# Other accumulation banks for the gate blocks of a feed-forward stage, and an up product placed one step earlier

## The chip, the cores and the metric

The kernel runs on one core of a Trainium2 chip. The time is that of one execution on the device, in microseconds (us), and the figure compared is the median of several executions. The engines of the core are called TensorE (PE in the profile, with its weight loads as PEld), VectorE (DVE), ScalarE (ACT), GpSimd (POOL) and SyncE (SP, which issues the DMAs).

## The reference

One encoder layer is applied to two token sequences of 256 and 512 tokens (768 rows, model width 1024) that share one set of weights, all in 32-bit floats. An input projection feeds three groups of heads, whose joined output goes through an output projection and a layer norm. The second half of the layer, on which the change bears, is

```
x = LN(alpha * x + mix)
h = silu(x @ w_gate) * (x @ w_up)          # 1024 -> 2816
y = LN(alpha * x + h @ w_down)             # 2816 -> 1024
```

with `alpha` the fourth root of 2. The result is the 768 x 1024 output, handed back as the two sequences.

## The kernel before

**Precision.** Each 32-bit operand is split in two reduced-precision parts, a high and a low one: ScalarE writes the high part (the cast of line 120), VectorE or GpSimd subtracts it from the source (line 121). Each product is three matmuls: high x high, high x low, low x high.

**Tiling of the feed-forward stage.** The 2816 hidden columns are 22 tiles of 128, taken as 11 pairs. The first pair (0) is computed plainly. For pairs 1 to 10 the four blocks of a gate or up product (two halves of the tokens by two tiles, over two halves of the model width) are computed with seven block products instead of eight, in Strassen's manner; they bear the numbers 1, 2, 6, 5, 7, 3, 4. `g1` to `g7` are the gate products of a pair, `u1` to `u7` the up products, `d1` to `d7` the seven products of the down projection, which run one pair behind. A gate or up product is 12 matmuls of 384 columns, a down product 9 matmuls of 512 columns: three token tiles t of three matmuls each. The last two pairs' down projection is done plainly at the end (`piece`, lines 1073 to 1094).

**Banks.** A PSUM bank holds one accumulation. `bank(i)` (line 925) gives banks 0 to 3 (tiles named `ff` in the profile), 4 and 5 (`sc`), 6 (`tp`) and 7 (`av`). In `gate_up` (lines 1007 to 1044) the three entries of `banks` are used so: the first holds products 1, 6, 7 and 4, which are added up one on the other; the second holds product 2; the third holds products 5 and 3. The up products get only two banks, 0 and 1, and then 5 and 3 share the second with product 2. Between two products in one bank the sum so far is taken out. Products 1, 6 and 5 are copied by ScalarE (`snap`, line 1031); products 2, 7 and 3 are read by VectorE, which adds such a copy (line 1040); product 4 of a gate is read by ScalarE's SiLU (line 943), product 4 of an up block by VectorE's multiplication with the SiLU (line 946). The next product may write the bank only when that read is done.
`down` (lines 1049 to 1067) uses banks 2, 3, 4 for products 1, 6, 7, 4 and banks 5, 6, 7 for products 2, 5, 3, one bank for each t, and VectorE adds each product onto `y` (line 1063).

**After an up block.** `gated` (line 945) multiplies and splits. When blocks 0, 1 and 3 are there (after u3), GpSimd forms `S1 = HB1 + HB3` (line 955), then new HB1 and HB0 (lines 956, 957), and after u4 new HB2 (line 959). ScalarE and VectorE split these into the `mix` tiles that the down products read (`gt_split`, and `gated_rest` after the pair).

**Order.** TensorE works strictly in the order written in the program, here the list `MIXED` (line 35), one pair after the other. The order on the other engines is not written out: a planner in the framework replays the program with its own model of durations and picks for each engine, among what is ready there, what stands earliest in the program. The order that it finds is then fixed, and each engine works it off in that order. After each product `op_done` (line 218) calls `pump`, which emits the next weight splits, in the order of `SPLIT_ORDER` (line 33), at most two after a gate or up product and none after a down product (`AHEAD`), behind the last line-1040 addition on VectorE. Five slots hold two split operands each; a slot is free when both of its products are done. Raw weights come in 512 KB loads through three buffers.

Of the kernel before, what the change touches and what calls it, by code (L numbers as in the profile page):

```python
# [31 lines left out]

SPLIT_ORDER = ("g1", "g2", "g6", "g5", "g7", "g3", "d1", "g4", "d2", "d6", "u1", "d5", "u2", "d7", "d3", "u6", "d4",
               "u5", "u7", "u3", "u4")
MIXED = ("g1", "g2", "g6", "g5", "g7", "g3", "d1", "g4", "d2", "u1", "d6", "u2", "d5", "u6", "d7", "u5", "d3",
         "u7", "d4", "u3", "u4")
OUT_ORDER = [6, 7, 2, 3, 4, 0, 1, 5]

# [26 lines left out]
def encoder_layer(ctx: ExitStack, tc, a, o):  # L65
# [35 lines left out]
    def run(main):  # L101
        for cost, f in main:
            catch_up(clock["now"])
            f()
            clock["now"] += cost
# [112 lines left out]
    def op_done(key, prod):  # L218
        n = w_tiles.pop((key, prod))[1]
        ops_done.add(n)  # L220

        while w_state["tail"] in ops_done and (w_state["tail"] + 1 in ops_done or w_state["tail"] == len(items) - 1):
            w_state["tail"] += 2
            w_state["free"] += 1
        if w_state.get("after") is None:
            pump()
        else:
            with tc.issue_after(w_state["after"]):
                pump(AHEAD[key[0]])
# [582 lines left out]
    def x1_block(name, m, k):  # L812
        if name in ("t3", "t4"):
            return mix[k + (4 if name == "t3" else 0)][:, m, :H2]
        return xb[name][:, m, k]
# [109 lines left out]
    def bank(i):  # L925
        if i < 4:
            return pff.tile([P, 512], F32, tag=f"p{i}", name="ff")
        return ps_one({4: "sc", 5: "sc", 6: "tp", 7: "av"}[i])
# [16 lines left out]
    def gated(i, src, p):  # L945
        V.tensor_tensor(out=HB[i], in0=src, in1=TH[i], op=ALU.mult)  # L946
        if p >= NP_ST:
            gt_split(4 * (p - NP_ST) + i, HB[i])
            return

        if i in (0, 2):
            gt_split(i // 2, HB[i])
        have.add(i)
        if i > 0 and {0, 1, 3} <= have and i != 2:
            G.tensor_tensor(out=S1, in0=HB[1], in1=HB[3], op=ALU.add)
            G.tensor_tensor(out=HB[1], in0=HB[0], in1=HB[1], op=ALU.subtract)
            G.tensor_tensor(out=HB[0], in0=S1, in1=HB[0], op=ALU.subtract)
        if len(have) == 4:
            G.tensor_tensor(out=HB[2], in0=HB[2], in1=HB[0], op=ALU.subtract)
            gt_split(2, HB[0])  # L960
            gt_split(3, S1)
            have.clear()
# [3 lines left out]
    def gated_rest():  # L966
        gt_split(4, HB[1])
        gt_split(5, HB[2])
        gt_split(6, HB[3])
# [37 lines left out]
    def gate_up(kind, p, banks):  # L1007
        st = {}

        def step(prod, k):  # L1010
            if k == 0 and prod < 3:
                st[prod] = bank(banks[prod - 1])[:, :H2]
                if prod == 2:
                    st[5] = st[2]
            elif k == 0 and prod == 5 and len(banks) > 2:
                st[5] = bank(banks[2])[:, :H2]
            b = st[{2: 2, 5: 5, 3: 5}.get(prod, 1)]
            w = w_tiles[(kind, p), prod][0]
            for wi, m in ((0, 0), (0, 1), (1, 0)):
                TE.matmul(b, lhsT=w[:, wi, k * P:(k + 1) * P], rhs=x1_block(x_name[prod], m, k),  # L1020
                          start=(prod in (1, 2, 5) and k == 0 and wi == 0 and m == 0), stop=(k == 3 and wi == 1), skip_group_check=prod in (6, 7, 4, 3))
            if k == 3:
                after(prod)
                op_done((kind, p), prod)

        def after(prod):
            use = silu if kind == "g" else lambda i, src: gated(i, src, p)
            out = TH if kind == "g" else HB
            if prod in (1, 6, 5):
                st["s", prod] = t = wk2.tile([P, H2], F32, tag="snap", name="snap", bufs=2)  # L1030
                snap = S.copy(out=t, in_=st[5 if prod == 5 else 1])  # L1031
                if prod == 6 and kind == "g":

                    with tc.issue_after(snap.ins):
                        use(0, out[0])
            elif prod == 4:
                use(2, st[1])
            else:
                i, b, other = {2: (0, 2, 1), 7: (3, 1, 5), 3: (1, 5, 6)}[prod]
                w_state["after"] = V.tensor_tensor(out=out[i], in0=st[b], in1=st["s", other], op=ALU.add).ins  # L1040
                if prod != 2 or kind == "u":
                    use(i, out[i])

        return lambda prods: [(0.48, lambda prod=prod, k=k: step(prod, k)) for prod in prods for k in range(4)]
# [4 lines left out]
    def down(p):  # L1049
        st = {}  # L1050

        def step(prod, t):
            if prod < 3:
                st[prod, t] = bank(2 + t if prod == 1 else 5 + t)
            b = st[1 if prod in (1, 6, 7, 4) else 2, t]
            w = w_tiles[("d", p), prod][0]
            for m, wi in ((0, 0), (0, 1), (1, 0)):
                TE.matmul(b, lhsT=gt_block(a_slot[prod], m)[:, t * P:(t + 1) * P], rhs=w[:, wi],  # L1058
                          start=(prod in (1, 2, 5) and m == 0 and wi == 0), stop=(m == 1),
                          skip_group_check=prod in (6, 7, 4, 3))  # L1060
            for dt, c in {1: ((0, lo_half),), 2: ((0, lo_half),), 6: ((0, hi_half),), 5: ((3, hi_half),),
                          7: ((3, hi_half),), 3: ((0, hi_half),), 4: ((3, lo_half),)}[prod]:
                V.tensor_tensor(out=y[t + dt][:, c], in0=b, in1=y[t + dt][:, c], op=ALU.add)
            if t == 2:
                op_done(("d", p), prod)

        return lambda prods: [(0.64, lambda prod=prod, t=t: step(prod, t)) for prod in prods for t in range(3)]
# [47 lines left out]
    run(first_pair())  # L1115
    gated_rest()
    for p in range(1, NP):
        g = gate_up("g", p, (0, 1, 7))
        if p <= NP_ST:
            part = {"g": g, "u": gate_up("u", p, (0, 1)), "d": down(p - 1)}  # L1120
            for m in MIXED:
                run(part[m[0]]((int(m[1]),)))
            if p < NP_ST:
                gated_rest()
        else:
            u = gate_up("u", p, (2, 3))
            run(g(PRODUCTS))
            run(u(PRODUCTS))
# [112 lines left out]
```

## Time and profile before

| | |
|---|---|
| time, 3 runs | median 894.96 us (894.76 to 895.37) |
| the profiled execution's own time | 893.65 us |
| its span in the profile | 891.9 us, so 1.75 us lie around the span |
| busy TensorE matmul, weight load | 848.9 us (95%), 761.2 us (85%) |
| busy VectorE, ScalarE, GpSimd | 647.6 us (73%), 421.9 us (47%), 380.5 us (43%) |
| matmul groups of `gate_up` (line 1020), first start to last | 393.8 to 851.0 us of the span |
| first gate product of pairs 1 to 10 starts at | 393.8, 443.0, 489.7, 537.4, 584.3, 632.9, 679.6, 727.1, 773.4, 821.8 us |

The profile is that of one execution. Its rows give for each instruction, or run of like instructions, when it started, how long the engine was busy with it, and where the engine sat idle just before, how long and what ended that idle time (`[1.51 <-DVE bv L946]`: 1.51 us, ended by the VectorE instruction of line 946 that writes `bv`). The 25 us steps of the page's overview hide stalls of one or two microseconds; the timeline of one engine shows them. The stage of the change is read pair by pair: from one first gate product to the next.

### The profile page before, as it was taken

How to read it: one execution, taken by the hardware profiler on the slowest of the kernel's cores; microseconds unless marked ns; L12 is line 12 of the kernel's file. 1: busy time of each engine (PE TensorE's matmuls, PEld its weight loads, DVE VectorE, ACT ScalarE, POOL GpSimd, SP SyncE). 2: the span in 40 equal slices, each digit the busy share in tenths (PEclk: the TensorE clock that was granted, in tenths of full speed). 3: DMA queues.
4: the chain of work that ended last, by engine and by line, in shares of the span. 5: the costliest groups of instructions: out<-in, count | busy, mean ns of one | idle time of the engine just before them, and what ended most of it. 6: DMA issues, size and time to landing. Idle time of an engine off the chain costs nothing. (4 is left out here: it accounts for less than half of the span.)

```text
span 891.9 us, 12951 instructions
## 1 busy us (share of the span) xinstructions
PE 848.9 (95%) x4811; PEld 761.2 (85%) x4811; DVE 647.6 (73%) x1168; ACT 421.9 (47%) x922; POOL 380.5 (43%) x320
## 2 busy tenths in 40 slices
PE   8999999999999998899999999989998999999996
PEld 6889897888987887798898998988897989898985
DVE  3564447576677568758888698878887888779577
ACT  3475476676665436544453434443434344344421
POOL 0670011100220148775564646456564465544235
PEclk9999999999999999999999999999999999999999
DMA  7830202011017202011212122122121212112222
GB/s 228 254 99 24 71 26 71 24 49 49 13 59 260 72 1 70 25 48 48 95 48 75 44 71 95 48 72 72 54 88 48 94 49 95 48 50 92 72 83 107
DMA packets 22160, 66.66 MB, mean 75 GB/s; under 512 B 3664, under 2 KB 5584, under 8 KB 22096
## 3 DMA queue, kind: packets, MB, share of 16 engines
q1 hardware_dynamic: 22096, 65.82, 21.9%
q8 instruction: 38, 0.62, 0.3%
q14 instruction: 26, 0.21, 0.1%
HBM read 62.67 MB, written 3.15 MB: 74 GB/s over the span
## 5 line engine op out<-in xcount | busy, mean ns | idle before, releaser
L121 DVE TENSOR_TENSOR w<-raw,w 128x512 fp32r<-128x512 f32 (+2 forms) x179 | 174.8, 994 | 56.1 <-ACT w L120 56.0
L120 ACT CAST w<-raw 128x512 fp32r<-128x512 f32 (+2 forms) x213 | 139.4, 676 | 124.2 <-PE sc L1058 41.2
L1020 PE MATMUL ff<-x,w 128*128 128x384 f32 x600 | 117.4, 348 | 19.6 <-DVE bv L946 16.9
L1020 PEld LDWEIGHTS ff<-x,w 128*128 128x128 f32 x600 | 109.5, 195 | 26.2 <-DVE bv L946 19.8
L1020 PE MATMUL ff<-mix,w 128*128 128x384 f32 x480 | 91.2, 338 | 1.9 <-ACT snap L1031 1.5
L1020 PEld LDWEIGHTS ff<-mix,w 128*128 128x128 f32 x480 | 84.4, 188 | 5.3 <-ACT snap L1031 3.1
L454 PE MATMUL mm<-xhi,w 128*128 128x512 f32 x320 | 79.0, 346 | 0.0
L175 POOL TENSOR_TENSOR raw<-raw 128x512 f32<-128x512 f32 x49 | 73.4, 1498 | 3.4 <-DVE w L121 0.7
L120 ACT CAST mix<-bv 128x384 fp32r<-128x384 f32 x62 | 31.8, 513 | 90.4 <-DVE bv L946 63.7
L121 POOL TENSOR_TENSOR w<-raw,w 128x512 fp32r<-128x512 f32 x34 | 49.8, 1473 | 55.7 <-ACT w L120 55.7
L433 PE MATMUL mm<-w,xhi 128*128 128x256 f32 x384 | 71.4, 286 | 0.0
L852 PE MATMUL mm<-w,mix 128*128 128x512 f32 x270 | 68.3, 399 | 1.5 <-ACT tt L696 0.8
L1020 PE MATMUL ff<-xt,w 128*128 128x384 f32 x360 | 67.7, 336 | 0.3 <-ACT snap L1031 0.3
L1020 PEld LDWEIGHTS ff<-xt,w 128*128 128x128 f32 x360 | 63.5, 188 | 2.1 <-ACT snap L1031 0.6
L121 DVE TENSOR_TENSOR mix<-bv,mix 128x384 fp32r<-128x384 f32 x62 | 55.1, 891 | 12.0 <-ACT mix L120 11.5
L631 POOL TENSOR_TENSOR mn<-mn,neghalf 128x1 f32<-128x1 f32 x24 | 13.7, 573 | 116.4 <-DVE mn L630 112.5
L175 POOL TENSOR_TENSOR ws<-raw 128x512 f32<-128x512 f32 x29 | 42.4, 1464 | 49.2 <-DMA raw<-in_w 44.9
L852 PEld LDWEIGHTS mm<-w,mix 128*128 128x128 f32 x270 | 49.2, 188 | 12.6 <-ACT tt L696 1.3
L433 PEld LDWEIGHTS mm<-w,xhi 128*128 128x128 f32 x384 | 58.1, 189 | 1.4 <-issue 0.9
L1058 PE MATMUL ff<-w,mix 128*128 128x512 f32 x216 | 55.7, 393 | 0.0
L454 PEld LDWEIGHTS mm<-xhi,w 128*128 128x128 f32 x320 | 49.0, 189 | 6.1 <-issue 0.7
L1058 PE MATMUL sc<-w,mix 128*128 128x512 f32 x189 | 53.8, 393 | 0.0
(234 smaller groups left out, 1777.8 us busy)
## 6 DMA issues: line engine op xcount, KB each, us to landing
raw<-in_w SPq DMA_DIRECT2D x95, 512.0 KB, 3.3
y<-in_x SPq DMA_DIRECT2D x6, 512.0 KB, 8.7
out_y<-y SPq DMA_DIRECT2D x12, 256.0 KB, 2.0
raw<-in_xT SPq DMA_DIRECT2D x7, 384.0 KB, 5.2
ln<-in_lng SPq DMA_DIRECT2D x2, 512.0 KB, 7.0
ln<-in_lnb SPq DMA_DIRECT2D x2, 512.0 KB, 7.6
rpb<-in_rpbs SPq DMA_DIRECT2D x32, 30.6 KB, 3.4
rpb<-in_rpbp SPq DMA_DIRECT2D x16, 59.6 KB, 2.8
```

What stands on the lines that cost most here:

```text
L120: S.copy(out=hi, in_=src)
L121: eng.tensor_tensor(out=lo, in0=src, in1=hi.bitcast(F32), op=ALU.subtract)
L175: G.tensor_tensor(out=out, in0=in0, in1=in1, op=f)
L433: TE.matmul(ps, lhsT=x[:, k, t * P:(t + 1) * P], rhs=w[:, wi, sl], start=(k == 0 and x is xhi and wi == 0), stop=(k == KT - 1 and x is xlo))
L454: TE.matmul(p, lhsT=w[:, wi, sl], rhs=x[:, k, c0:c1], start=(k == 0 and wi == 0 and x is x_hi), stop=(k == KT - 1 and wi == 1))
L631: G.tensor_tensor(out=mn[:, 7:8], in0=mn[:, 7:8], in1=neghalf[:, 0:1], op=ALU.pow)
L852: TE.matmul(ps, lhsT=mix[OUT_ORDER[i]][:, m, t * P:(t + 1) * P], rhs=w[:, wi, sl], start=(i == first and m == 0 and wi == 0), stop=(i == l ...
L1020: TE.matmul(b, lhsT=w[:, wi, k * P:(k + 1) * P], rhs=x1_block(x_name[prod], m, k), start=(prod in (1, 2, 5) and k == 0 and wi == 0 and m = ...
L1058: TE.matmul(b, lhsT=gt_block(a_slot[prod], m)[:, t * P:(t + 1) * P], rhs=w[:, wi], start=(prod in (1, 2, 5) and m == 0 and wi == 0), stop= ...
```

## The change

Two edits. The gate blocks of pairs 1 to 10 get the banks 7, 1, 0 in place of 0, 1, 7: products 1, 6, 7 and 4 now gather in bank 7, products 5 and 3 in bank 0, product 2 stays in bank 1. And in TensorE's order the first up product goes in front of the second down product. `SPLIT_ORDER`, the order in which weights are split, stays.

```diff
 MIXED = ("g1", "g2", "g6", "g5", "g7", "g3", "d1", "g4", 
-         "d2", "u1", "d6", "u2", "d5", "u6", "d7", "u5", "d3",
+         "u1", "d2", "d6", "u2", "d5", "u6", "d7", "u5", "d3",
          "u7", "d4", "u3", "u4")
...
     for p in range(1, NP):
-        g = gate_up("g", p, (0, 1, 7))
+        g = gate_up("g", p, (7, 1, 0))
```

## Rows read from the trace of the kernel before

**Rows 1.** Waits of TensorE: us in total, times, longest.
```profile
PE ff L1020 <- DVE bv L946: 16.9, 9, 2.2
PE ff L1020 <- ACT ffs L943: 2.1, 2, 1.3
PE ff L1020 <- ACT snap L1031: 1.7, 4, 1.1
PE mm L852 <- DVE w L121: 0.6, 1, 0.6
```
**Rows 2.** TensorE timeline, end of pair 1 into pair 2: start, busy, count, idle before.
```profile
439.24 2.25 PE L1020 MATMUL ff<-mix,w 128*128 128x384 f32 x12
443.00 4.49 PE L1020 MATMUL ff<-x,w 128*128 128x384 f32 x24 [1.51 <-DVE bv L946]
...
451.57 2.28 PE L1020 MATMUL ff<-mix,w 128*128 128x384 f32 x12
```
**Rows 3.** TensorE timeline, end of pair 2 into pair 3.
```profile
485.25 2.24 PE L1020 MATMUL ff<-mix,w 128*128 128x384 f32 x12
489.68 6.01 PE L1020 MATMUL ff<-x,w 128*128 128x384 f32 x24 [2.19 <-DVE bv L946]
...
499.97 2.38 PE L1020 MATMUL ff<-mix,w 128*128 128x384 f32 x12
```
**Rows 4.** TensorE's granted clock (PEclk) in a window just after that wait.
```profile
490.50:491.50 1.00, 1.00 (x5) 1.00 (x4) 0.27 (x1) 0.63 (x2) 0.60 (x1) 0.50 1.02 283
```
**Rows 5.** TensorE timeline, end of pair 6 into pair 7.
```profile
675.14 2.28 PE L1020 MATMUL ff<-mix,w 128*128 128x384 f32 x12
679.56 4.43 PE L1020 MATMUL ff<-x,w 128*128 128x384 f32 x24 [2.14 <-DVE bv L946]
...
689.76 2.37 PE L1020 MATMUL ff<-mix,w 128*128 128x384 f32 x12 [1.07 <-ACT snap L1031]
```
**Rows 6.** TensorE timeline, end of pair 9 into pair 10.
```profile
817.39 2.25 PE L1020 MATMUL ff<-mix,w 128*128 128x384 f32 x12
821.76 4.43 PE L1020 MATMUL ff<-x,w 128*128 128x384 f32 x24 [2.13 <-DVE bv L946]
...
830.24 2.28 PE L1020 MATMUL ff<-mix,w 128*128 128x384 f32 x12
```
**Rows 7.** VectorE timeline, end of pair 2.
```profile
486.21 2.48 DVE L121 TENSOR_TENSOR w<-raw,w 128x512 fp32r<-128x512 f32 x4
488.61 0.55 DVE L946 TENSOR_TENSOR bv<-bv,ffs 128x384 f32<-128x384 f32 x1
489.08 0.55 DVE L946 TENSOR_TENSOR bv<-ff,ffs 128x384 f32<-128x384 f32 x1
```
**Rows 8.** GpSimd timeline, start of pair 3.
```profile
495.13 1.32 POOL L957 TENSOR_TENSOR bv<-gs,bv 128x384 f32<-128x384 f32 x1
```
**Rows 9.** ScalarE timeline, start of pair 3.
```profile
496.49 0.51 ACT L120 CAST mix<-bv 128x384 fp32r<-128x384 f32 x1 [2.10 <-POOL bv L957]
...
499.03 0.52 ACT L120 CAST mix<-bv 128x384 fp32r<-128x384 f32 x1 [0.99 <-POOL bv L959]
499.45 0.47 ACT L1031 COPY snap<-ff 128x384 f32<-128x384 f32 x1
```
**Rows 10.** ScalarE timeline, start of pair 2.
```profile
449.93 0.51 ACT L120 CAST mix<-bv 128x384 fp32r<-128x384 f32 x1 [2.54 <-POOL bv L957]
450.35 0.47 ACT L1031 COPY snap<-ff 128x384 f32<-128x384 f32 x1
```
**Rows 11.** ScalarE timeline, pair 3, around the SiLU of product g4.
```profile
509.54 0.62 ACT L120 CAST w<-raw 128x512 fp32r<-128x512 f32 x1 [3.95 <-POOL raw L175]
510.06 0.48 ACT L943 ACTIVATE ffs<-ff 128x384 f32<-128x384 f32 x1
```
**Rows 12.** VectorE timeline, pair 3: the low half of u1's weights.
```profile
498.51 1.03 DVE L121 TENSOR_TENSOR w<-raw,w 128x512 fp32r<-128x512 f32 x1
```
**Rows 13.** Pair 3 whole: PE, PEld, DVE, ACT, POOL busy, PEclk, DMA share, GB/s.
```profile
489.68:537.42 47.74, 46.18 (x231) 42.61 (x231) 39.16 (x56) 19.79 (x39) 26.65 (x20) 0.96 0.20 67
```

More of the change, by code (lines that the diff above doesn't have):

```diff
@@ L34 @@
                "u5", "u7", "u3", "u4")
-MIXED = ("g1", "g2", "g6", "g5", "g7", "g3", "d1", "g4", "d2", "u1", "d6", "u2", "d5", "u6", "d7", "u5", "d3",
+MIXED = ("g1", "g2", "g6", "g5", "g7", "g3", "d1", "g4", "u1", "d2", "d6", "u2", "d5", "u6", "d7", "u5", "d3",
          "u7", "d4", "u3", "u4")
```

## The prediction

> **What bounds the kernel now.** I read the page first (TensorE 95% busy, so only its idle time can be won), then TensorE's waits, then its timeline at each change of pair, and last the timelines of VectorE, GpSimd and ScalarE there. In the feed-forward stage TensorE has one large wait: nine times, once at the end of each pair 1 to 9, the first gate product sits until VectorE has multiplied the last up block [rows 1]. The reason is the bank: g1 opens bank 0, and u4 has just been gathered in bank 0; the multiplication that reads it stands on VectorE behind four weight splits and the multiplication for u3 [rows 7]. The wait is 1.48 to 1.56 us where an odd pair ends (four times, the first shown [rows 2]) and 2.13 to 2.19 us where pairs 2, 4, 6, 8 and 9 end [rows 3, 5, 6]. After three of the five long waits the granted clock is 0.50, the level of 1.2 GHz [rows 4], and g1 with g2 take 6.0 instead of 4.4 us [rows 3, 5].
>
> The sum of the waits, 16.9 us, is not what the edit is worth. A better measure is the way from the start of u4 to the start of g7, in which u4, g1, g2, g6 and g5 run. Without any wait a product takes 2.12 us: g1 to g7 in pair 10 are 8.48 us for four [rows 6]. So the way is 10.6 us at least. It is 12.33 us into pair 2 [rows 2] and 12.18 to 12.27 into pairs 4, 6 and 8; 14.72 into pair 3 [rows 3], 14.62 into pair 7 [rows 5], 14.78 and 14.84 into pairs 5 and 9; 12.85 into pair 10 [rows 6]. That pairs 3, 5, 7 and 9 agree is the point to see: pair 7 had no low clock and yet is not earlier, since it then waited 1.07 us at g7 for ScalarE's copy of g6 [rows 5]. In pair 3 that copy ends at 499.92 and g7 starts at 499.97, close behind it [rows 3, 9]. So a second chain ends there at nearly the same time: VectorE's multiplications, GpSimd's combinations up to lines 957 and 959, ScalarE's casts of what these give, and behind them, in ScalarE's queue, the copy of g6 that g7 needs, because g7 adds onto g6 in the same bank [rows 7 to 9].
>
> **The change part by part.** *Banks.* Nothing is added: the same matmuls, copies, additions and SiLUs run. g1 now opens bank 7, which d3 used last; between d3 and g1 stand u7, d4, u3 and u4, more than 8 us, so its reading is long done, and the wait of g1 goes. Bank 0 is opened by g5 instead, three products (6.4 us) after g1. The multiplication ended at 489.63 in pair 3 [rows 7], and g5 would come at 485.25 + 4 x 2.12 = 493.7, so it does not wait. g2 stays in bank 1, which u3 left a product earlier.
> What is late next is the copy of g6. Lower bound of the gain: ScalarE's order stays, g7 starts at 499.97 as now, and nothing is won into pairs 3, 5, 7, 9. Upper bound: g7 comes 10.6 us after u4 everywhere. That is 4 x (14.74 - 10.6) = 16.6 us for the pairs 3 to 9, 4 x (12.25 - 10.6) = 6.6 for 2 to 8, and 2.25 for pair 10: 25.4 us.
> Which of them? The planner gives ScalarE the order by what is ready first in its own replay, and there too g1 loses its wait, so the copy of g6 becomes ready earlier by 1.5 to 2.3 us against the GpSimd chain, which hangs on u3 and VectorE and not on g1. Today the copy stands behind both casts in pair 3 [rows 9] and between them in pair 2 [rows 10]; the two are 2.54 us apart [rows 9]. In pair 2 it was ready when g6 ended, near 451.57 - 2.12 = 449.45, some 0.5 us ahead of the earlier cast's start; a shift of 1.7 us widens that. In pair 3 g6 ended near 489.68 + 5.9 + 2.1 = 497.7, 1.2 us behind the earlier cast's start; the shift there is the wait of 2.2 us and, where the replay has it too, 1.5 of slow clock. I take: in front of both. Then g7 is on time, and the copy of g5, which g3 needs, is next: it stands behind the line-957 cast (done at 497.00 in pair 3 [rows 9]) and, I assume, two weight casts of 0.52 us step each, so it is done near 498.4, and g3 is due at 485.25 + 12.7 = 498.0. That costs about 0.45 us in the five long cases, 2.3 us in all, and nothing in the short ones.
> *u1 in front of d2.* Without this edit d2's third tile, in bank 7, would come only 1.4 us after g4 and wait for g4's SiLU; now it comes 2.1 + 1.4 = 3.5 us after. u1 in its turn no longer waits for that SiLU, since bank 0 was left by g3: the two waits on line 943, 2.1 us in all, go [rows 1]. Against it: in pair 3 the SiLU ran at 510.06 to 510.54, because it stood behind a weight cast that waited for GpSimd's sums of freshly loaded weights [rows 11]. g4 ended near 508.4, so 2.1 us after; today that is inside the 3.5. If TensorE is 3.7 us earlier there and that cast is not, d2's third tile is due at 508.3 and waits 2.2 us, in pairs 3, 5, 7 and 9: 9 us at most, 0 if the SiLU is put in front of the cast. I take a third of it, 3 us, since the SiLU becomes ready earlier by as much as TensorE gains.
> *Weights.* u1 is needed 2.1 us sooner than its place in the split order gives. In pair 3 its split ended at 499.54 [rows 12] and it started at 510.60; with 2.1 for the move and 3.7 for the gain some 5 us remain. In even pairs the emission of three pairs of splits (u5 with u7, u3 with u4, g1 with g2) falls one or two steps later, as the slot of g4 and d2 is freed one product later. TensorE never waits for a split in this stage (the only such wait is in the output projection [rows 1]), so I cost this at nothing. The raw loads behind these splits keep their order; no wait of SP's queue is added. VectorE is busy 39 of 48 us in a pair [rows 13]; at 45 us it still fits.
> Sum: 16.6 + 6.6 + 2.25 + 2.1 - 2.3 - 3 = 22.2 us. The profiled execution took 893.65 us, span 891.9; it becomes 871.5. The median is 1.3 us above the profiled execution, so 873.
>
> **The rivals.** *A, the copy of g6 passes only the later cast.* In pairs 3 to 9 it ends at 496.49 + 0.51 + 0.47 = 497.5 [rows 9], the way is 12.2, and 2.5 us are won four times; into pairs 2 to 8 it ends as now at 450.82 [rows 10], the way is 11.6, 0.6 won four times; 1 in pair 10, 2.1 at the SiLU: 15.5 us, so 879.5. For it: in both kinds of pair the line-957 cast stands in front today.
> *B, ScalarE's order stays as it is.* The wait moves from g1 to g7 in pairs 3 to 9: 0 there, 2.5 into the even pairs, 1 and 2.1 as above. But TensorE then stands idle 4.1 us in one piece, and if the clock falls after each of these, as after three of five waits of 2.1 us, 1.6 us of slow matmuls [rows 3, 4] come four times on top, now behind the chain and not hidden by it: +0.8, so 895.8, no measurable change.
> The Trainium skill (PSUM — Partial Sum Buffer, section on engine and sequencer instructions) says that the queues of ScalarE, VectorE and GpSimd are strictly first in, first out. The trace agrees: the copy of g6, ready near 497.7 in pair 3, ran at 499.45 behind a cast that waited [rows 9]. By that rule alone, with the order unchanged, the outcome would be B's; it is the reason why freeing a bank need not free TensorE.
> *C, slower.* B's mechanism with a longer chain: the later emission puts g1's and g2's splits into the block of four that stands in front of the multiplication for u3 at the end of the even pairs [rows 7]. Two more are 1.25 us on the chain, with the slow clock 2.85 us, four times 11.4, less the 5.6 that B keeps: +5.8, so 901. It decides from 1.4 us a pair on.
> *D, no effect*: bank 7 comes free as late as bank 0 did. Its last reader is 8 us old; I see nothing for it. 895.
>
> **How the numbers follow.** Forecast 0.55 (867 to 877, the two assumed costs at nothing or at full), A 0.23 (877 to 882), B 0.12, C 0.07, D 0.03. The range is 866 to 889: it holds the forecast and A and leaves out most of B, C and D. What a measurement of this kernel can tell from no change is 0.2%, 1.8 us. Faster: 0.55 + 0.23 + 0.06 of B (with the clock held up) = 0.84; the same: 0.08; slower: 0.08.
>
> **What would show it.** Right: no wait of g1 on line 946; g7 about 10.6 to 11 us after u4; pairs of 44.5 to 45.5 us instead of 46.3 to 48.7; PEclk 1.00 at the changes of pair; no wait of u1 on line 943. On ScalarE the copy of g6 in front of both casts. For A or B: g7 waits on the copy, 1 to 4 us. Wrong: a new wait of d2 in `av` on line 943, a matmul of line 1020 waiting for a split, or ways from u4 to g7 that stay at 14.7.

## The result, and the profile after

The changed kernel takes 870.28 us (869.17 to 871.16) where the kernel before took 894.86 us in the same comparison: 0.9726 of it, interval 0.9709 to 0.9742. The forecast was 873.0 in a range of 866 to 889. The profiled execution went from 893.65 to 870.31 us, its span from 891.9 to 868.5.

TensorE's waits after the change (us in total, times, longest). The nine waits on line 946 of [rows 1] are gone, and so are the two on line 943; the new entry is the first line: five waits of a product in bank 7 (`av`) for VectorE's addition of line 1040.

```profile
PE av L1020 <- DVE ffs L1040: 3.6, 5, 0.8
PE ff L1020 <- DVE bv L1001: 1.7, 1, 1.7
PE ff L1020 <- ACT snap L1031: 0.5, 2, 0.3
```

TensorE's timeline, end of pair 2 into pair 3, to be held against [rows 3] (start, busy, idle before). From u4 in the first line to g7 in the third it is 10.56 us instead of 14.72, and g1 follows u4 after 2.08 us. The last line is g4 with the new wait.

```profile
483.27 2.24 PE L1020 MATMUL ff<-mix,w 128*128 128x384 f32 x12
485.35 2.28 PE L1020 MATMUL av<-x,w 128*128 128x384 f32 x12
...
493.83 2.24 PE L1020 MATMUL av<-mix,w 128*128 128x384 f32 x12
...
501.06 2.35 PE L1020 MATMUL av<-mix,w 128*128 128x384 f32 x12 [0.82 <-DVE ffs L1040]
```

Pairs 2 and 3 whole (the second answers to [rows 13]; busy PE, PEld, DVE, ACT, POOL, then PEclk): TensorE is busy without a gap in pair 2, the granted clock is 1.00, and VectorE is busy 43 of 45 us in pair 3.

```profile
441.33:485.35 44.02, 44.02 (x232) 41.14 (x232) 38.90 (x56) 19.84 (x38) 26.78 (x19) 1.00 0.22 72
485.35:530.41 45.06, 44.24 (x232) 41.17 (x232) 42.95 (x58) 19.54 (x38) 28.06 (x19) 1.00 0.21 71
```

ScalarE's timeline, start of pair 3, against [rows 9]: the copy of g6 (first line) now stands in front of the cast that waits for line 957. The last line is the SiLU of g4, which starts as g4 ends (503.41; compare [rows 11]).

```profile
492.14 0.47 ACT L1031 COPY snap<-av 128x384 f32<-128x384 f32 x1
...
494.85 0.52 ACT L120 CAST mix<-bv 128x384 fp32r<-128x384 f32 x1 [1.81 <-POOL bv L957]
495.27 0.47 ACT L1031 COPY snap<-ff 128x384 f32<-128x384 f32 x1
...
503.46 0.49 ACT L943 ACTIVATE ffs<-av 128x384 f32<-128x384 f32 x1 [0.54 <-PE av L1020]
```

Where the span's 23.4 us came from, from the starts of the products in both traces: the nine ways from u4 to g7 went from 120.8 to 94.3 us, 26.5 won; from g4 to u2, where the waits for the SiLU sat, 78.2 to 76.1, 2.1 won; from g7 to d1 39.4 to 38.9, 0.5 won; from d1 to g4 19.2 to 23.8, 4.6 lost. Pair 1 lost 0.9 between g1 and g7, where g2 waited 1.7 instead of 0.7 us for the first pair's line 1001; in a second profile of the changed kernel it waits 0.7 again, so this loss is that execution's. The rest, 0.4 lost, is the later start of the stage, in this execution too.

### The profile page after: what moved, and what is told of

The parts are those of the page before. It is cut to its first block, busy times and chain, and to the rows that moved or that the text cites. A ratio compares the mean times of both kernels' runs of the same rounds, so it can differ in the third digit from the quotient of the medians.

```text
span 868.5 us, 12944 instructions
## 1 busy us (share of the span) xinstructions
PE 841.2 (97%) x4811; PEld 756.5 (87%) x4811; DVE 664.5 (77%) x1168; ACT 422.0 (49%) x922; POOL 387.6 (45%) x320
## 5 line engine op out<-in xcount | busy, mean ns | idle before, releaser
L121 DVE TENSOR_TENSOR w<-raw,w 128x512 fp32r<-128x512 f32 (+2 forms) x179 | 184.4, 1051 | 43.4 <-ACT w L120 43.3
L1020 PE MATMUL ff<-x,w 128*128 128x384 f32 x600 | 113.3, 337 | 2.2 <-DVE bv L1001 1.7
L1020 PEld LDWEIGHTS ff<-x,w 128*128 128x128 f32 x600 | 105.5, 188 | 4.9 <-DVE bv L1001 2.0
L175 POOL TENSOR_TENSOR raw<-raw 128x512 f32<-128x512 f32 x49 | 75.2, 1535 | 3.4 <-DVE w L121 0.7
L121 DVE TENSOR_TENSOR mix<-bv,mix 128x384 fp32r<-128x384 f32 x62 | 60.9, 995 | 10.3 <-ACT mix L120 10.1
L852 PEld LDWEIGHTS mm<-w,mix 128*128 128x128 f32 x270 | 49.2, 188 | 12.5 <-ACT tt L696 1.3
L433 PE MATMUL mm<-w,xlo 128*128 128x256 f32 x192 | 53.4, 278 | 0.0
L1020 PE MATMUL av<-mix,w 128*128 128x384 f32 x240 | 46.1, 340 | 3.8 <-DVE ffs L1040 3.6
```

The costliest lines, as they stand in the source:

```text
L121: eng.tensor_tensor(out=lo, in0=src, in1=hi.bitcast(F32), op=ALU.subtract)
L175: G.tensor_tensor(out=out, in0=in0, in1=in1, op=f)
L433: TE.matmul(ps, lhsT=x[:, k, t * P:(t + 1) * P], rhs=w[:, wi, sl], start=(k == 0 and x is xhi and wi == 0), stop=(k == KT - 1 and x is xlo))
L852: TE.matmul(ps, lhsT=mix[OUT_ORDER[i]][:, m, t * P:(t + 1) * P], rhs=w[:, wi, sl], start=(i == first and m == 0 and wi == 0), stop=(i == l ...
```

## Experiments

Each edit is against the changed kernel, unless it says otherwise.

**1. The banks alone** (the kernel before, with only this):

```diff
-        g = gate_up("g", p, (0, 1, 7))
+        g = gate_up("g", p, (7, 1, 0))
```

> Gate blocks in banks 7, 1, 0, u1 left behind d2. My theory: nearly the whole gain is the banks. d2's third tile is now due 1.4 us after g4; where ScalarE's SiLU of g4 runs at once (done 0.7 us after g4, as after the change) it does not wait: 870 us, at most 873. Rival (the reason I gave for the second edit in the prediction): the SiLU stands late in ScalarE's queue and d2 in the av bank waits on line 943, 0.7 us or more in each of nine pairs: 876 us or more.

Measured: 871.46 us, 0.9732 of before (0.9704 to 0.9759). The first expectation holds. d2 waits for the SiLU once, in pair 1:

```profile
PE av L1058 <- ACT ffs L943: 1.9, 1, 1.9
```

So the banks, with the orders that the planner then gives the other engines, are the gain, and the second edit is worth too little to be measured in whole times. The traces do show it: from g4 to u2 the nine pairs take 78.4 us here, 78.2 before and 76.1 after the whole change.

**2. The move alone** (u1 in front of d2, banks 0, 1, 7).

> u1 in front of d2, gate blocks left in banks 0, 1, 7. My theory: the nine waits of g1 on line 946 stay (16 to 17 us), and u1, now right behind g4 in the same bank 0, waits for g4's SiLU in every pair, 0.7 us at least and 2 us or more where the SiLU is late: slower than before, 900 to 910 us. Rival: the move alone wins the 2.1 us of waits on line 943: 893 us.

Measured: 911.87 us, 1.0183 of before (1.0155 to 1.0211), slower, as the theory had it and 2 us beyond its upper end. The waits on line 946 stay, and u1 waits behind g4's SiLU in bank 0 in every pair:

```profile
PE ff L1020 <- DVE bv L946: 16.9, 9, 2.2
PE ff L1020 <- ACT ffs L943: 15.0, 9, 3.4
```

**3. Both edits, with ScalarE's old order.** The copy of g6 is queued behind the cast behind which it stood before.

```diff
+                if prod == 6 and kind == "g" and p <= NP_ST:
+                    with tc.issue_after(cast[2 if p % 2 == 0 else 5].ins):
+                        snap = S.copy(out=t, in_=st[1])
```

(`cast[i]` is the high-part cast of down operand i; 2 hangs on line 957, 5 on line 959.)

> Both edits of the change, but ScalarE's copy of g6 is held in its queue behind the casts that it stood behind before the change: the one that waits for line 957 in even pairs, for line 959 in odd pairs. My theory (a freed bank is worth nothing while that copy stands behind GpSimd's chain): the way from u4 to g7 goes back to 14 to 15 us into odd pairs and 11.5 to 12 into even ones, with waits of g7 on the copy of 4 and 1 us: 886 to 896 us. Rival (the wait of g1 was the cost, the copy's place in the queue matters little): 870 to 875 us.

Measured: 910.22 us, 1.0168 of before (1.0136 to 1.0199). The rival is out: the freed bank brings nothing while the copy stands there. But it is 14 us more than my upper end. The ways from u4 to g7 are 11.6 us into even pairs, as foreseen, and 16.9 to 17.0 into odd ones. TensorE, GpSimd and ScalarE timelines and a window of the clock, start of pair 3 (u4 at 490.41):

```profile
507.39 4.21 PE L1022 MATMUL av<-mix,w 128*128 128x384 f32 x12 [6.25 <-ACT snap L1035]
```
```profile
501.90 1.71 POOL L188 TENSOR_TENSOR ws<-raw 128x512 f32<-128x512 f32 x1
503.57 1.57 POOL L176 TENSOR_TENSOR raw<-raw 128x512 f32<-128x512 f32 x1
505.11 1.30 POOL L960 TENSOR_TENSOR bv<-bv 128x384 f32<-128x384 f32 x1
```
```profile
506.44 0.51 ACT L120 CAST mix<-bv 128x384 fp32r<-128x384 f32 x1 [2.18 <-POOL bv L960]
506.86 0.47 ACT L1035 COPY snap<-av 128x384 f32<-128x384 f32 x1
```
```profile
507.50:509.00 1.50, 1.50 (x5) 1.50 (x6) 0.53 (x2) 0.62 (x2) 0.57 (x1) 0.50 0.20 79
```

Three things were not in my expectation. GpSimd's order had changed as well: between lines 957 and 959 (958 and 960 here) stand two sums of raw weights instead of one, so that the chain from u4 to the cast ends 16.5 us after u4, where [rows 9] has 14.3. The hold did not do this: the order came with the banks. The changed kernel has it too, in pair 3 (u4 at 483.27), but there the copy of g6 does not stand behind it:

```profile
494.78 1.75 POOL L187 TENSOR_TENSOR ws<-raw 128x512 f32<-128x512 f32 x1
496.50 1.60 POOL L175 TENSOR_TENSOR raw<-raw 128x512 f32<-128x512 f32 x1
498.06 1.33 POOL L959 TENSOR_TENSOR bv<-bv 128x384 f32<-128x384 f32 x1
```

Then, the granted clock is 0.50 (1.2 GHz) after the idle 6.25 us. And in pair 1 the hold does not restore the old order: before the change the copy of g6 stood in front of both casts there, and g7 did not wait, while here it waits 6.37 us. ScalarE before, pair 1:

```profile
402.78 0.47 ACT L1031 COPY snap<-ff 128x384 f32<-128x384 f32 x1
...
404.76 0.52 ACT L120 CAST mix<-bv 128x384 fp32r<-128x384 f32 x1 [1.08 <-POOL bv L957]
```

The ways cost 30.5 us against the changed kernel, pair 1 another 5.6, the stretches from g7 to u4, with the slow matmuls in them, 4.9. Against the kernel before, pair 1 costs 6.4 us from g1 to g7 and GpSimd's longer chain 8.9 in the four odd ways (67.8 us against 58.9). Without these two, 910.2 would be near 895, by an estimate from these rows: the bank without the copy's new place is worth nothing, and the 15 us lost are not its own.

**4. The old banks with ScalarE's new order** (the kernel before; the splits of operands 2 and 5 are emitted behind the copy of g6).

```diff
-            gt_split(2, HB[0])
+            held.append(lambda: gt_split(2, HB[0]))
...
-        gt_split(5, HB[2])
+        held.append(lambda: gt_split(5, HB[2]))
...
+                if prod == 6 and kind == "g":
+                    with tc.issue_after(snap.ins):
+                        while held:
+                            held.pop(0)()
```

> Banks and order of TensorE as before the change; on ScalarE the copy of g6 is put in front of both casts. My theory: g1 keeps its waits of 1.5 and 2.2 us, so the way from u4 to g7 is these plus 10.6, 12.3 into even pairs (no gain) and 12.9 to 14.4 into odd ones (the latter where the clock falls): 888 to 894 us. Rival (ScalarE's queue was the whole cost): 875 to 880 us.

Measured: 893.02 us, 0.9979 of before (0.9964 to 0.9994). As the theory had it. g1 has its waits, 16.9 us in nine; the ways into odd pairs are 13.4 (pair 5, where the clock stays at 1.00) to 14.5 us: the wait, the fall of the clock, and the products. Into pair 3 (u4 at 486.20, g7 at 500.64, no wait of g7 any more):

```profile
490.63 6.01 PE L1021 MATMUL ff<-x,w 128*128 128x384 f32 x24 [2.19 <-DVE bv L946]
...
500.64 1.55 PE L1021 MATMUL ff<-mix,w 128*128 128x384 f32 x8
```

Experiments 3 and 4 with the kernels before and after make a square: old bank and old queue 894.9, new queue alone 893.0, new bank alone 910.2, both 870.3. It is not a clean one: the third corner holds pair 1's hold and GpSimd's other order (near 895 without them, as estimated above), and the last two have the moved u1, which changes whole times too little to be measured beside the new banks (experiment 1).

**5. The copy behind the first cast only** (as 3, with `cast[2]` in all pairs).

> Both edits of the change, ScalarE's copy of g6 held only behind the cast that waits for line 957, in all pairs: what the prediction's rival A supposes. Theory: the way from u4 to g7 is 11.6 us into even pairs, as in e3_new_banks_old_queue, and 12 to 12.5 into odd ones, no fall of the clock: 8 to 16 us above the changed kernel with pair 1's share, 878 to 886 us. Rival (any hold costs as much as in e3_new_banks_old_queue, since a hold delays more than the copy): 895 us or more.

Measured: 882.51 us, 0.9876 of before (0.9842 to 0.9910). Ways of 11.6 to 11.8 us into even pairs, 12.4 to 12.5 into odd ones; TensorE waits nine times on the copy:

```profile
PE av L1022 <- ACT snap L1035: 13.8, 9, 2.4
```

It is the prediction's rival A, priced at 879.5 there; the longest wait, 2.4 us, is that of pair 1, which rival A does not have.

**6. Another order of the same banks**, (7, 0, 1).

> The changed kernel with gate blocks in banks 7, 0, 1: g2 opens bank 0 instead of g5. The multiplication that leaves bank 0 ends 3.7 us after the start of u4 where an odd pair ends and 4.4 where an even one does; g2 is due at 4.2. Theory (it only matters that the first product's bank is free; bank 0 is late by at most 0.2 us for the second): waits of g2 of 0 to 0.4 us, 870 to 872 us. Rival (any gate product that opens bank 0 early brings the old stall back): 880 us or more.

Measured: 871.82 us, 0.9735 of before (0.9715 to 0.9755). Three waits on line 946 are back, of 0.7 us at most, more than the 0.4 foreseen:

```profile
PE av L1020 <- DVE ffs L1040: 2.4, 6, 0.6
PE ff L1020 <- DVE bv L946: 2.0, 3, 0.7
```

It is the first product's bank that counts; one product later bank 0 is nearly free.

**7. What is left: VectorE in front of g4.** VectorE's timeline in pair 3 of the changed kernel. The addition that reads g7 (`av`, line 1040), which could run from 496 on, runs at 500.47, behind splits that take 1.5 to 1.6 us each.

```profile
495.29 3.22 DVE L121 TENSOR_TENSOR mix<-bv,mix 128x384 fp32r<-128x384 f32 x2
498.44 1.50 DVE L121 TENSOR_TENSOR w<-raw,w 128x512 fp32r<-128x512 f32 x1
499.87 0.68 DVE L121 TENSOR_TENSOR w<-ws,w 128x512 fp32r<-128x512 f32 x1
500.47 0.54 DVE L1040 TENSOR_TENSOR ffs<-av,snap 128x384 f32<-128x384 f32 x1
```

The experiment leaves GpSimd's sums and differences of raw weights out of the computation.

```diff
-                for out, in0, in1, f in steps:
-                    G.tensor_tensor(out=out, in0=in0, in1=in1, op=f)
...
-                src = w_sum[key]
+                src = r[1][:, first]
...
-            G.tensor_tensor(out=w_sum[key], in0=r[1][:, second], in1=r[0][:, second], op=ALU.subtract)
```

> The changed kernel without GpSimd's sums and differences of raw weights (lines 175 and 187 left out; the products that used them take raw weights instead, the split of weights stays). Theory (GpSimd's reading of SBUF is what lengthens VectorE's splits): the mean of line 121 on VectorE in the stage falls from 1.03 to 1.06 us towards 0.7 us, that of lines 1063 and 1040 stays at 0.67 and 0.55, g4's wait on line 1040 goes: 864 to 867 us. Rival (VectorE's splits are long for another reason, or they are not what g4 waits for): the means stay above 0.95 us and the wait stays: 869 us or more.

Measured: 861.26 us, 0.962 of before (0.9603 to 0.9637), below my range. No wait of TensorE in the stage is left, pairs take 43.7 to 44.0 us. VectorE's groups in the stage, by shape (count, busy us, mean ns), of the kernel before, of the changed one, and of this one (line 1047 here is line 1063; its 144 weight splits include 32 that read `ws` in the other two):

```profile
L121 DVE TENSOR_TENSOR w<-raw,w 128x512 fp32r<-128x512 f32 x113 | 107.3, 968 | 24.4 <-ACT w L120 24.4
L121 DVE TENSOR_TENSOR mix<-bv,mix 128x384 fp32r<-128x384 f32 x49 | 44.7, 914 | 11.1 <-ACT mix L120 10.9
L1063 DVE TENSOR_TENSOR y<-ff,y 128x512 f32<-128x512 f32 x64 | 41.2, 677 | 0.6
```
```profile
L121 DVE TENSOR_TENSOR w<-raw,w 128x512 fp32r<-128x512 f32 x114 | 115.1, 1032 | 10.1 <-ACT w L120 10.1
L121 DVE TENSOR_TENSOR mix<-bv,mix 128x384 fp32r<-128x384 f32 x48 | 49.8, 1051 | 8.1 <-ACT mix L120 8.1
L1063 DVE TENSOR_TENSOR y<-ff,y 128x512 f32<-128x512 f32 x64 | 41.1, 675 | 0.0
```
```profile
L121 DVE TENSOR_TENSOR w<-raw,w 128x512 fp32r<-128x512 f32 x144 | 104.8, 765 | 8.0 <-ACT w L120 7.9
L121 DVE TENSOR_TENSOR mix<-bv,mix 128x384 fp32r<-128x384 f32 x48 | 39.4, 827 | 2.3 <-ACT mix L120 2.3
L1047 DVE TENSOR_TENSOR y<-ff,y 128x512 f32<-128x512 f32 x64 | 42.5, 686 | 1.1
```

The splits read two operands from SBUF, and their means fall with GpSimd's load, though not to the 0.7 us of my expectation; the additions that read one operand from PSUM stay at 0.68 to 0.69 us. One trace of the changed kernel shows the same without an experiment. Of the `w<-raw,w` splits that start in the window of the second view, 53 overlap no GpSimd instruction and take 0.67 to 0.68 us each; the other 60 overlap one and take 1.35 us in the mean. In the rows above, the split at 498.44 runs beside GpSimd's line 959 (498.06 to 499.39) and takes 1.50 us; the one at 499.87 has no GpSimd instruction beside it and takes 0.68. The Trainium skill (SBUF — State Buffer, section on who interferes with whom) says that a VectorE instruction with two SBUF inputs contends with a GpSimd instruction that reads SBUF, and one with at most one SBUF input does not; these rows agree. The time itself is no clean price of it, since without the sums ScalarE's casts no longer wait for them either.

**8. and 9. The four splits that hang on GpSimd behind the addition of g7, or of g3.** They (`gt_split` of operands 2, 4, 5 and 6) are held back and emitted under a queue order on VectorE. The diff is that of 8; in 9 it says `prod == 3`. In the texts below, 8 is called e5_splits_behind_g7 and 9 e8_splits_behind_g3.

```diff
+                if prod == 7 and kind == "g":
+                    with tc.issue_after(w_state["after"]):
+                        while held:
+                            held.pop(0)()
```

> The changed kernel, with four splits of the down operands (those that hang on lines 956, 957 and 959, and the one of block 3) queued on VectorE behind the addition that reads g7. Theory: what is left of waiting in the changed kernel, 0.8 us of g4 in each of pairs 1, 3, 5, 7 and 9, comes from VectorE working off two of these splits at 1.6 us each in front of that addition; with them behind it the wait goes and d1 to g4 takes 2.1 us again: 866 to 868 us. Rival: the weight splits in front of the addition are late as well, or the splits are now late for d6, d7 and d3, and nothing is won: 870 us or more.

Measured: 867.55 us, 0.9693 of before (0.9676 to 0.9709). g4's wait is gone in all pairs; in its place u1 waited for g3's addition, in three pairs:

```profile
PE ff L1021 <- DVE ffs L1041: 3.4, 3, 2.0
```

> As e5_splits_behind_g7, but the four splits stand on VectorE behind the addition that reads g3, two products later. Theory: the waits that came in their place there (u1, which opens bank 0 after g3, waited 3.4 us in three pairs for that addition behind the splits) go too, and the splits are still in time for d6, d7, d3 and d4: 863 to 866 us, pairs of 44.0 us. Rival: they come too late for d6 or push VectorE's additions onto y, and TensorE waits there: 868 us or more.

Measured: 868.30 us, 0.9702 (0.9678 to 0.9725), above the range I gave, where the rival had put it, but not for the rival's reason: those waits went, no down product waited for its splits, and in their place the copy of g1, which g6 needs, was late at the start of the even pairs (g6 waited 0.71, 0.28, 0.15 and 0.18 us in pairs 2, 4, 6 and 8; the fifth wait below is g7's in pair 1).

```profile
PE av L1021 <- ACT snap L1032: 1.5, 5, 0.7
```

All three kernels then ran once more, side by side:

> The changed kernel once more, on the same chip as the two next to it: 0.972 to 0.974 of before.

> e5_splits_behind_g7 on the same chip: its stage from g1 of pair 1 to g1 of pair 10 was 2.1 us shorter than the changed kernel's, so 2 to 3 us below it. Rival: the difference was one of chips, and it is within 1 us.

> e8_splits_behind_g3 on the same chip: the same stage was 5.4 us shorter than the changed kernel's, but its start came 1.8 us later, which I take for the spread of the first stages: 3 to 5 us below the changed kernel. Rival: the later start belongs to the kernel, and it is 2 us below it, as e5.

Measured: changed kernel 870.58 us, 0.9731 (0.9718 to 0.9745); splits behind g7 866.58 us, 0.9686 (0.9673 to 0.9699); behind g3 866.69 us, 0.9695 (0.9680 to 0.9709). Both are 4 us faster than the changed kernel, the first by more than the 2 to 3 expected; between the two there is no difference that these runs can tell. In the second profile of the first of them, u1 waited in pair 1 alone, so its waits in pairs 3 and 5 differ from one execution to the next.

## Why the prediction was right, point by point

**The measure.** The way from u4 to g7 was the right thing to count. The forecast of 25.4 us for nine ways at 10.6 us stands against 26.5 us measured; they are 10.40 to 10.56 us, since a product takes 2.08 to 2.12. Pairs 2 to 9 take 44.0 to 45.5 us, against 44.5 to 45.5 foreseen.

**The bank.** No wait of g1 is left, and g5 in bank 0 does not wait. By itself this is not the gain: in experiment 3 the same banks win nothing (what they lose there has two other sources), and experiment 4 shows that the queue without the bank gives 2 us.

**The copy of g6.** The prediction took it that the planner would put the copy in front of both casts. It did, in pairs 2 to 9, and in pair 3 in front of the line-957 cast by 2.7 us (492.14 against 494.85). This was the step on which the outcome hung, and it was argued, not seen; A and B were its failures. A was priced at 879.5 and measures 882.5 in experiment 5, with a wait in pair 1 that A does not have. B's price, 895.8, went by today's chain; experiment 3 comes near it only by the estimate without pair 1 and without GpSimd's new order, and no run shows that corner clean. What I had not foreseen is that the planner rearranges GpSimd too. C, priced at 901 for a longer chain, had such a lengthening, though another than this one.

**The mis-sized terms.** 2.3 us were set for g3 behind the copy of g5: it waits 0.5 us in all, in pairs 1 and 9 (in the second profile 0.8, in pairs 1 and 3). In pair 3 of the first profile it does not wait, because the copy (495.27) comes straight behind the line-957 cast, not behind two weight casts. 3 us were set for d2's third tile behind the SiLU: nothing, the SiLU starts within 0.3 us of g4's end in pairs 2 to 9, and 2.9 us after it in pair 1, inside the 3.5 that the move leaves. What was lost instead, 4.6 us from d1 to g4, I had not named: bank 7 holds g7 too, and its reader, the addition of line 1040, stands in VectorE's queue. The 5.3 us set and the 5.1 us lost cancel nearly; the total was right partly by that, which is luck. The 1.3 us added because the median before lay above the profiled execution were not there after (870.28 and 870.31).

**The second edit.** The prediction credits it with the 2.1 us of waits on line 943 and says that without it d2 would wait for the SiLU. Experiment 1 has one such wait, 1.9 us in pair 1, and no measurably different time. In the traces the 2.1 us are the move's: without it the way from g4 to u2 stays at 78.4 us (u1's wait of 1.3 us in pair 1 becomes one of d2), with it it is 76.1. The expectation that d2 would wait in the other pairs too is not borne out. Without the new banks the move costs 17 us.

**Covers.** No product of the stage waited for a weight split in any of these traces, as forecast. VectorE "still fits" was half right: it is busy 43 of 45 us in pair 3, and the last waits, those of g4 on line 1040, are in the odd pairs.

## What to carry to other kernels

Where a wait on a buffer is to be removed, find what the waiting engine meets next and follow that chain to its own start: the gain is the difference of the two, and by the estimate of experiment 3 the freed bank in front of the old queue wins nothing. Measure it between two fixed points of the program that span both waits, not by the wait itself. Where a planner orders the other engines, the order it will choose is part of the forecast, and holding one instruction in its old place is the experiment that shows its worth, once the other engines' orders are compared too: here GpSimd's had changed with the bank, and one pair was held that had been free.

## What the runs showed of the hardware that I had not expected

VectorE's splits lengthened as the stage grew shorter, with the same work: 968 to 1032 ns and 914 to 1051 ns, while its PSUM-reading additions stayed at 675 to 677 ns. A weight split of 0.68 us takes 1.35 us in the mean beside a GpSimd instruction (experiment 7), so VectorE's busy time itself depends on how GpSimd's instructions fall beside it. In pair 3 it rose from 39.2 [rows 13] to 42.95 us; a pair that seemed to have 8.6 us of room had 2.1.
